# A hybrid block on one Trainium2 core: inverse's products emitted later among the dense matmuls, and an output projection that holds three weight tiles

## The chip, the core and the metric

The kernel runs on one core of one Trainium2 chip. The engines have separate, in-order instruction streams: TensorE (PE in the profile, with its weight loads as PEld), VectorE (DVE), ScalarE (ACT), GpSimd (POOL) and SyncE (SP). Semaphores, set by a tile framework, make one stream wait for another. The metric is device microseconds of one execution. The time of this kernel is 1151.71 us, the median of three runs that lie between 1146.16 and 1154.17 us.

## What is computed

One layer for 512 tokens of width 1024: a pre-norm, three token mixers, a gated merge, an output projection with residual, and a squared-ReLU MLP with residual and a last norm. Cut to what matters here:

```python
h = rms_norm(x, norm1_g)
p = h @ w_in                      # 1024 -> 11520 columns
y_a = b_a * causal_dwconv(c_a * x_a)                 # short convolution
y_b = rg_lru(causal_dwconv(x_b)) * gelu(g_b)         # linear recurrence over tokens
# RWKV-7, 16 heads of 64; state carried over 8 chunks of 64 tokens
sa = state @ (-kk); state = state*w + sa (kk*a)^T + v k^T; y_t = state @ r
m = gate_a*y_a + gate_b*y_b + gate_c*y_c
x = x + m @ w_out                 # 1024 x 1024
h2 = rms_norm(x, norm2_g)
x = x + square(relu(h2 @ mlp_w1)) @ mlp_w2           # 1024 -> 4096 -> 1024
return rms_norm(x, final_g)
```

## The kernel before, in words

All float32 products are made of three matmuls of split operands (`mm3`, lines 166 to 169): a high part and a low part of weight and of data. A weight tile is 128 x 1024. `load_w` (line 132) fetches it on SP's queue into `raw` (two buffers), ScalarE casts it to `whi` (line 146) and VectorE makes `wlo` = `raw` - `whi` (line 103, the helper `tt`). `whi` and `wlo` have three buffers each, so a tile can be split only when the matmuls of the third tile before it are done. A projection of one weight tile is 24 matmuls of 128x512 on TensorE; these are called dense matmuls below.

The RWKV mixer works on four groups of four heads. For each group `krv` (line 415) makes keys, decays, receptances and values; `amat` (line 514) makes the small products between them within each chunk (`pA`, then the transposes `pB`); `inverse` (line 543) inverts 32 triangular blocks of 64 by 64. Two `v.transpose` (line 550) bring the blocks' halves into `Z`, 31 steps of two short VectorE operations each (`dg` and `Z`, lines 559 and 561) invert the diagonal 32 by 32 blocks, two more transposes (line 567) and one (line 572) bring the result into the layout that TensorE needs, and 32 + 32 small matmuls (`pG`, line 577, and `pT`, line 587, in blocks of 16) make the off-diagonal part. Line 569 yields NINV times ahead of line 572, so that other work is emitted in between.

Everything else of the input projection (the branches `ab`, line 734: 8 times 7 weight tiles and the recurrences) is filler: a generator `fl` that `weave` (line 813) advances by a given number of steps for each step of the critical generator. The order in which instructions are emitted, with the priority offsets that `tc.high_priority` sets (CP, CPI and so on), is what the framework's scheduler turns into one fixed order on each engine. A matmul emitted under `pin` keeps its emission order and has a high priority.

After the last inverse the recurrence over eight chunks runs (`chain`, line 618), with the rest of the filler and the gates (`gate`, line 716) between its steps. Then `fin_m` (line 698) merges the branches, four steps for the first 256 tokens and four for the rest: for each of two row blocks q it makes `ym`, its high part `mh` (ScalarE) and its low part `ml` (VectorE). `w_out(th)` (line 873) multiplies them with the eight tiles of `w_out`, once for each half of the tokens, 24 matmuls of 128x256 for a tile and half; `to_tokens` (line 887) transposes the residual stream back and stores it. The MLP follows (`p`, then `acc` with `ah`).

Of the kernel before, what the change touches and what calls it, by code (L numbers as in the profile page):

```python
# [18 lines left out]
P = 128  # L19

OFF, OFFS, OFFP = 160, 20, 30
CP, CPI, CPK, CPC, CPN = 150, 60, 0, 20, 5
HOT = 6000

NINV, NG_T, N_LOAD = 16, 4, 6


N_INV, N_KRV = 41, 22
F_INV, F_KRV, F_GAP = 29, 14, 5
R0, R2, R3, R4 = 0.85, 0.8, 1.6, 1.0  # L30
NWARM = 2
POOL_KT = (1, 3, 5, 6, 7)
S = 512
# [64 lines left out]
def block_kernel(ctx, tc, xt, win, par, mulr, sw, wout, w1, w2, fg, cst, eyes, out):  # L98
# [3 lines left out]
    def tt(o, a, b, op):  # L102
        return v.tensor_tensor(out=o, in0=a, in1=b, op=op)  # L103
# [410 lines left out]
    def amat(g, G_):  # L514

        G_.AX = p1.tile([P, 2, NC, 4, L], F32, tag="AXt", name="AXt")
        for c4 in range(2):
            pts = four_banks("pA")
            for i in range(16):
                ci, jj, h = i // 4, 1 - i // 2 % 2, i % 2  # L520
                c = 4 * c4 + ci
                rows = slice(64 * h, 64 * h + 64)
                pin(i, lambda: pe.matmul(pts[2 * h + jj][:, ci], G_.BK[rows, jj, c], G_.AR[rows, jj, c],  # L523
                                 start=True, stop=True))
            for e in range(4):
                tt(G_.AX[:, :, 4 * c4:4 * c4 + 4, e], pts[e].rearrange("p c (a t) -> p a c t", a=2),
                   mask.rearrange("p (a t) -> p a t", a=2).unsqueeze(2).to_broadcast([P, 2, 4, L]), MUL)
            yield
        gp.dma_start(axd[:, 0:64, g, 1].rearrange("c s e t -> s c (e t)"),
                     G_.AX[0:64, 1].rearrange("s c e t -> s c (e t)"))  # L530
        for a in range(2):
            gp.dma_start(axd[:, 64:128, g, a].rearrange("c s e t -> s c (e t)"),
                         G_.AX[64:128, a].rearrange("s c e t -> s c (e t)"))
        BKT = p1.tile([P, NC, 2, P], F32, tag="BKT", name="BKT")
        for c2, pt in enumerate(four_banks("pB")):
            for i in range(4):
                c, jj = 2 * c2 + i // 2, i % 2
                pin(c2 + i, lambda: pe.transpose(pt[:, i], G_.BK[:, jj, c].rearrange("p a t -> p (a t)"), ident))
            ac.copy(BKT[:, 2 * c2:2 * c2 + 2].rearrange("p c j t -> p (c j) t"), pt)
        gp.dma_start(bkd[:, :, g].rearrange("c p j x -> p c (j x)"), BKT.rearrange("p c j x -> p c (j x)"))  # L540
        yield

    def inverse(g, G_):
        AXt = G_.AX
        Z = p1.tile([P, 2, 32, 32], F32, tag="Z", name="Z")
        la, xt = Z[64:128, 0], Z[64:128, 1]
        dg = p1.tile([P, 32, 32], F32, tag="dg", name="dg")
        tmp = dg[64:128].rearrange("p a b -> p (a b)")
        for b in range(2):
            v.transpose(la[32 * b:32 * b + 32].rearrange("l s t -> l t s"),  # L550
                        AXt[32 * b:32 * b + 32, 0, :, :, 32 * b:32 * b + 32].rearrange("s c e t -> s t (c e)"))
        gp.dma_start(xt.rearrange("l s t -> l (s t)"), eyes)

        yield
        yield
        for s in range(31):
            n, c = 31 - s, s + 1
            tv = tmp[:, 0:n * c].rearrange("l (c t) -> l c t", c=c)
            tt(tv, la[:, s, s + 1:32].unsqueeze(1).to_broadcast([64, c, n]),
               xt[:, 0:c, s:s + 1].to_broadcast([64, c, n]), MUL)  # L560
            tt(xt[:, 0:c, s + 1:32], xt[:, 0:c, s + 1:32], tv, ADD)
# [10 lines left out]
        v.transpose(d1[0:32], TT[0:32, :, 0:32])  # L572
        for half in range(2):
            pg = pm.tile([P, 16, 32], F32, tag="pm", name="pG")
            for i in range(16):
                l = 16 * half + i
                pin(i, lambda: pe.matmul(pg[32:64, i], AXt[0:32, 0, l // 4, l % 4, 32:64], d1[0:32, l],  # L577
                                             start=True, stop=True))
            ac.copy(gs[32:64, 16 * half:16 * half + 16], pg[32:64])
            yield  # L580
        for _ in range(NG_T):
            yield 0
        for half in range(2):
            pg = pm.tile([P, 16, 32], F32, tag="pm", name="pT")
            for i in range(16):
                l = 16 * half + i
                pin(i + half, lambda: pe.matmul(pg[0:32, i], gs[32:64, l], TT[32:64, l, 32:64], start=True, stop=True))
# [221 lines left out]
    def chainit(*gens):  # L809
        for x_ in gens:  # L810
            yield from x_
# [28 lines left out]
    pk_ctx.close()  # L840
# [12 lines left out]
    def fill_chain():  # L853
# [14 lines left out]
            yield  # L868
        yield from fin_m(0, 4)
        M["half"] = True  # L870
        yield from w_out(0)

    def w_out(th):
        tl = slice(th * HT, (th + 1) * HT)
        for mo in range(KT):
            w = load_w(wout[mo])
            acc = pp.tile([P, S], F32, tag="pp", name="acc")[:, 0:HT]
            for q in range(KT):
                mm3(acc, *wslice(w, q), GQ[q][th], BV[q][th], start=q == 0, stop=q == KT - 1)
            x2 = M["x2T"][:, mo, tl]  # L880
            tt(x2, acc, x2, ADD)
            hi = M["h2h"][:, mo, tl]
            ac.activation(hi, x2, AF.Copy, scale=pv("n2", mo))
            stt(M["h2l"][:, mo, tl], x2, pv("n2", mo), f(hi), MUL, SUB)
            yield

    def to_tokens(th):
# [195 lines left out]
```

## Time and profile before

| | |
|---|---|
| median of three runs | 1151.71 us (1146.16 to 1154.17) |
| the profiled execution | 1150.43 us, span of its instructions 1148.7 us |
| granted TensorE clock, mean | 0.955 |
| busy: TensorE, VectorE, ScalarE, GpSimd | 1071.1, 753.9, 484.2, 107.6 us |
| first pA of group 1 to the last pT of group 4 | about 86 to 592 us |
| chain over chunks | about 607 to 715 us |
| merge and output projection | about 724 to 789 us |
| MLP | about 789 to the end |

A row of the waits reads: engine, tile and line that waited, what released it, then us in total, times, longest. A row of the windows reads: the stretch in us from the span's start, its length, then busy us and number of instructions of TensorE, its weight loads, VectorE, ScalarE and GpSimd, the granted TensorE clock, the DMA engines' busy share and GB/s. A row of the timeline reads: start, duration, engine, line, operation, tiles; in brackets the idle time before it and what ended it. The profiler lists a small float32 matmul (pA, pG, pT) as two records, so 32 records of pG are a block of 16.

### The profile page before, as it was taken

To read this page: it belongs to the slowest core of one execution; us is meant where nothing else is said; L and a number is where in the kernel's file an instruction comes from. 1 tells how busy PE (TensorE), PEld (TensorE's weight loads), DVE (VectorE), ACT (ScalarE), POOL (GpSimd) and SP (SyncE) were. 2 spreads that over 40 slices of the span, in tenths; PEclk is the share of its full clock that TensorE was granted. 3 is DMA by queue.
4 is the path that set the end of the run, shared out by engine and by line. 5 is a ranking of instruction groups with operands and counts; after the bars stand their busy time and mean duration, and the time that the engine had idled before them with its cause. 6 is when DMAs were issued, how large, how long until landed. Compare 5 with 4: busy or idle time off the path is not lost.

```text
span 1148.7 us, 16170 instructions
## 1 busy us (share of the span) xinstructions
PE 1071.1 (93%) x6396; PEld 875.9 (76%) x6396; DVE 753.9 (66%) x1300; ACT 484.2 (42%) x714; POOL 107.6 (9%) x167
## 2 busy tenths in 40 slices
PE   8899969999699996999878999789999999999997
PEld 4677857788577875778667888689888888888885
DVE  7997967879579894898955777966544444222224
ACT  6645335444265451554525444355433433211123
POOL 3211001110011100001012220100000000000001
PEclk9999969999699996999979999889999999999999
DMA  6244414463234622436239873355333225323331
GB/s 207 81 126 123 149 55 114 114 158 116 59 99 140 173 78 80 115 114 175 76 110 288 265 236 116 129 177 182 101 97 105 92 93 178 115 92 95 107 92 73
DMA packets 44475, 146.32 MB, mean 127 GB/s; under 512 B 5808, under 2 KB 9392, under 8 KB 43376
## 3 DMA queue, kind: packets, MB, share of 16 engines
q1 hardware_dynamic: 30624, 95.21, 26.3%
q0 software_dynamic: 13056, 49.03, 14.9%
q8 instruction: 50, 0.82, 0.3%
q10 hardware_dynamic: 720, 1.05, 0.2%
q14 instruction: 25, 0.20, 0.1%
HBM read 120.11 MB, written 25.17 MB: 126 GB/s over the span
## 4 chain that ended last, share of the span: by engine, by line
PE 53%; DVE 10%; issue 7%; DMA 2%; ACT 1%; POOL 1%; ACTq 0%; POOLq 0%; DVEq 0%; SPq 0%
PE acc L167 6%; PE acc L168 6%; PE acc L169 6%; PE p L168 5%; PE p L167 5%; PE p L169 5%; PE pp L167 4%; PE pp L169 4%; PE pp L168 4%; DVE wlo L103 2%; DMA rt<-rtd 2%; PE py L644 1%; DVE dg L103 1%; DVE Z L103 1%; PE pA L523 1%
## 5 line engine op out<-in xcount | busy, mean ns | idle before, releaser
L103 DVE TENSOR_TENSOR wlo<-raw,whi 128x1024 fp32r<-128x1024 f32 (+1 forms) x172 | 209.5, 1219 | 274.1 <-ACT whi L146 260.4
L146 ACT CAST whi<-raw 128x1024 fp32r<-128x1024 f32 (+1 forms) x172 | 178.0, 1036 | 342.3 <-PE acc L169 126.2
L167 PE MATMUL pp<-hh,whi 128*128 128x512 f32 x696 | 270.9, 403 | 4.0 <-ACT g L747 1.1
L169 PE MATMUL pp<-hh,wlo 128*128 128x512 f32 x696 | 268.7, 400 | 4.2 <-DVE wlo L103 4.2
L168 PE MATMUL pp<-hl,whi 128*128 128x512 f32 x696 | 267.9, 399 | 2.8 <-DVE hl L106 2.8
L167 PEld LDWEIGHTS pp<-hh,whi 128*128 128x128 f32 x696 | 133.3, 192 | 36.0 <-ACT hh L291 1.5
L169 PEld LDWEIGHTS pp<-hh,wlo 128*128 128x128 f32 x696 | 133.3, 192 | 34.5 <-DVE wlo L103 6.0
L168 PEld LDWEIGHTS pp<-hl,whi 128*128 128x128 f32 x696 | 133.5, 192 | 31.5 <-DVE hl L106 3.2
L169 PE MATMUL p<-h2h,wlo 128*128 128x512 f32 (+1 forms) x264 | 101.2, 383 | 0.0
L167 PE MATMUL p<-h2h,whi 128*128 128x512 f32 (+1 forms) x264 | 101.1, 383 | 0.0
L168 PE MATMUL p<-h2l,whi 128*128 128x512 f32 (+1 forms) x264 | 101.0, 383 | 0.0
L167 PE MATMUL acc<-whi,ah 128*128 128x512 f32 x256 | 99.6, 389 | 0.0
L168 PE MATMUL acc<-wlo,ah 128*128 128x512 f32 x256 | 99.6, 389 | 0.0
L169 PE MATMUL acc<-whi,al 128*128 128x512 f32 x256 | 99.6, 389 | 0.0
L169 PEld LDWEIGHTS p<-h2h,wlo 128*128 128x128 f32 x264 | 49.6, 188 | 9.7
L167 PEld LDWEIGHTS p<-h2h,whi 128*128 128x128 f32 x264 | 49.6, 188 | 9.6
L168 PEld LDWEIGHTS p<-h2l,whi 128*128 128x128 f32 x264 | 49.6, 188 | 9.5
L168 PEld LDWEIGHTS acc<-wlo,ah 128*128 128x128 f32 x256 | 48.0, 188 | 10.1
L169 PEld LDWEIGHTS acc<-whi,al 128*128 128x128 f32 x256 | 48.0, 188 | 10.1
L167 PEld LDWEIGHTS acc<-whi,ah 128*128 128x128 f32 x256 | 48.0, 188 | 9.8
L577 PE MATMUL pG<-dg,AXt 32*32 32x32 f32 x256 | 14.7, 236 | 36.5 <-DVE dg L572 36.5
L103 DVE TENSOR_TENSOR dg<-Z 64x31 f32<-64x31 f32 (+15 forms) x124 | 42.2, 340 | 4.1
(296 smaller groups left out, 1519.9 us busy)
## 6 DMA issues: line engine op xcount, KB each, us to landing
raw<-in_win SPq DMA_DIRECT2D x88, 512.0 KB, 3.5
raw<-in_w SPq DMA_DIRECT2D x64, 512.0 KB, 3.5
ax<-axd POOLq DMA_DIRECT2D x8, 1024.0 KB, 8.0
raw<-in_wout SPq DMA_DIRECT2D x16, 512.0 KB, 3.5
axd<-AXt POOLq DMA_DIRECT2D x12, 512.0 KB, 7.4
bkd<-BKT POOLq DMA_DIRECT2D x4, 1024.0 KB, 13.9
bk<-bkd POOLq DMA_DIRECT2D x7, 512.0 KB, 9.5
swr<-in_sw SPq DMA_DIRECT2D x16, 128.0 KB, 2.3
```

The lines of the kernel that those rows point to most:

```text
L103: return v.tensor_tensor(out=o, in0=a, in1=b, op=op)
L146: ac.copy(hi[:, sl], raw[:, sl])
L167: pe.matmul(ps, wh, xh, start=start, stop=False)
L168: pe.matmul(ps, wh, xl, start=False, stop=False)
L169: pe.matmul(ps, wl, xh, start=False, stop=stop)
L523: pin(i, lambda: pe.matmul(pts[2 * h + jj][:, ci], G_.BK[rows, jj, c], G_.AR[rows, jj, c], start=True, stop=True))
L577: pin(i, lambda: pe.matmul(pg[32:64, i], AXt[0:32, 0, l // 4, l % 4, 32:64], d1[0:32, l], start=True, stop=True))
L644: pin(behind, lambda: pe.matmul(py[64 * h:64 * h + 64, x], w, y, start=first and x == 0, stop=last, skip_group_check=True))
```

## The change

Two things are changed. In the RWKV groups, the last transpose of `inverse` (`d1`) is emitted ahead of the yields and not behind them, there are 19 yields instead of 16, and they have no extra priority. Keys and filler of the next group are now one generator, `fill_group`, that runs beside the inverse (1.15 steps for each of its steps) and is drained behind it; before, the inverse ran beside filler alone and `krv` followed. All small matmuls of `pA` are pinned, the first one too. In the output projection, three weight tiles are held: `w_out_first` multiplies them with the first half of the tokens, into the left half of three PSUM tiles, and `w_out_rest` with the second half; the five other tiles are loaded once and multiplied with both halves. `to_tokens(0)` comes after that. So eight loads and splits of weight tiles go, and the additions behind the projection are 512 tokens wide.

```diff
-CP, CPI, CPK, CPC, CPN = 150, 60, 0, 20, 5
+CP, CPI, CPK, CPC, CPN = 150, 0, 0, 20, 5
-NINV, NG_T, N_LOAD = 16, 4, 6
-N_INV, N_KRV = 41, 22
-F_INV, F_KRV, F_GAP = 29, 14, 5
-R0, R2, R3, R4 = 0.85, 0.8, 1.6, 1.0
+NINV, NG_T, N_LOAD = 19, 4, 6
+N_KRV = 22
+F_INV, F_KRV, F_GAP = 22, 16, 4
+W3 = 3
+R0, R1, R2, R3, R4 = 0.85, 1.15, 1.1, 1.7, 1.0
...
-                pin(i, lambda: pe.matmul(pts[2 * h + jj][:, ci], G_.BK[rows, jj, c], G_.AR[rows, jj, c],
+                pin(True, lambda: pe.matmul(pts[2 * h + jj][:, ci], G_.BK[rows, jj, c], G_.AR[rows, jj, c],
...
+        d1 = gs = dg
+        v.transpose(d1[0:32], TT[0:32, :, 0:32])
         for _ in range(NINV):
             yield CPI
-        d1 = gs = dg
-        v.transpose(d1[0:32], TT[0:32, :, 0:32])
...
+    def fill_group(g):
+        for _ in range(F_INV):
+            next(fl, None)
+            yield
+        acc = 0.0
+        for _ in krv(g, GS[g]):
+            yield
+            acc += F_KRV / N_KRV
+            while acc >= 1.0:
+                acc -= 1.0
+                next(fl, None)
+                yield
+        for _ in range(F_GAP):
+            next(fl, None)
+            yield
...
         if g:
-            weave(inverse(g - 1, GS[g - 1]), fl, F_INV / N_INV)
-            weave(krv(g, GS[g]), fl, F_KRV / N_KRV, CPK)
-            for _ in range(F_GAP):
-                next(fl, None)
+            fgr = fill_group(g)
+            weave(inverse(g - 1, GS[g - 1]), fgr, R1)
+            drain(fgr)
...
-        yield from w_out(0)
+        yield from w_out_first()
...
+    def w_out_mm(mo, w, acc, th):
+        for q in range(KT):
+            mm3(acc[:, HALF[th]], *wslice(w, q), GQ[q][th], BV[q][th], start=q == 0, stop=q == KT - 1)
+    def w_out_first():
+        M["w"], M["acc"] = [], []
+        for mo in range(W3):
+            w = load_w(wout[mo])
+            acc = pp.tile([P, S], F32, tag="pp", name="acc")
+            w_out_mm(mo, w, acc, 0)
+            M["w"].append(w)
+            M["acc"].append(acc)
+            yield
+    def w_out_rest():
+        for mo in range(W3):
+            w_out_mm(mo, M["w"][mo], M["acc"][mo], 1)
+            w_out_end(mo, M["acc"][mo])
+            yield
+        for mo in range(W3, KT):
+            w = load_w(wout[mo])
+            acc = pp.tile([P, S], F32, tag="pp", name="acc")
+            for th in range(2):
+                w_out_mm(mo, w, acc, th)
+            w_out_end(mo, acc)
+            yield
...
+    drain(w_out_rest())
     drain(to_tokens(0))
-    drain(w_out(1))
```

What the scheduler makes of it is seen in the order of the instructions. Line numbers of the changed kernel are one higher from line 30 on, 571 is the `d1` transpose, and later ones are up to 39 higher. Numbers behind a name tell buffers of one name apart.

TensorE, the first group's inverse, before: the end of the dense matmuls in front of the first `pG`. `pp_1466` and `pp_1486` are two projections, each with its own `whi` and `wlo`.

```order
L167 MATMUL pp_1466<-hh_73,whi_1461 128x512
L167 MATMUL pp_1486<-hh_73,whi_1481 128x512
L168 MATMUL pp_1466<-hl_74,whi_1461 128x512
L168 MATMUL pp_1486<-hl_74,whi_1481 128x512
L169 MATMUL pp_1466<-hh_73,wlo_1462 128x512
L169 MATMUL pp_1486<-hh_73,wlo_1482 128x512
L167 MATMUL pp_1466<-hh_73,whi_1461 128x512
L167 MATMUL pp_1486<-hh_73,whi_1481 128x512
L577 MATMUL pG_1306<-dg_1038,AXt_927 32x32 x16
```

The same engine and place in the changed kernel: the 182nd to 187th dense matmul behind the last `pB`.

```order
L170 MATMUL pp_1414<-hh_73,wlo_1410 128x512
L168 MATMUL pp_1428<-hh_73,whi_1423 128x512
L169 MATMUL pp_1428<-hl_74,whi_1423 128x512
L170 MATMUL pp_1428<-hh_73,wlo_1424 128x512
L168 MATMUL pp_1428<-hh_73,whi_1423 128x512
L169 MATMUL pp_1428<-hl_74,whi_1423 128x512
```

And the `pG` block of the changed kernel, behind 260 dense matmuls:

```order
L170 MATMUL pp_1545<-hh_73,wlo_1541 128x512
L168 MATMUL pp_1545<-hh_73,whi_1540 128x512
L169 MATMUL pp_1545<-hl_74,whi_1540 128x512
L170 MATMUL pp_1545<-hh_73,wlo_1541 128x512
L578 MATMUL pG_1564<-dg_1038,AXt_927 32x32 x16
L168 MATMUL pp_1513<-hh_73,whi_1508 128x512
```

The small matmuls moved back by 78 dense ones in this group, and dense ones now stand between their blocks.

VectorE at the end of the same inverse, before:

```order
L103 TENSOR_TENSOR wlo_1482<-raw_1480,whi_1481 128x1024
L103 TENSOR_TENSOR Z_1037<-Z_1037,dg_1038 64x28x4
L103 TENSOR_TENSOR dg_1038<-Z_1037 64x87
L103 TENSOR_TENSOR Z_1037<-Z_1037,dg_1038 64x29x3
L103 TENSOR_TENSOR dg_1038<-Z_1037 64x60
L103 TENSOR_TENSOR Z_1037<-Z_1037,dg_1038 64x30x2
L103 TENSOR_TENSOR dg_1038<-Z_1037 64x31
L103 TENSOR_TENSOR Z_1037<-Z_1037,dg_1038 64x31
L567 STREAM_TRANSPOSE Z_1037<-Z_1037 32x32x32 x2
L572 STREAM_TRANSPOSE dg_1038<-Z_1037 32x1024
L103 TENSOR_TENSOR wlo_1541<-raw_1539,whi_1540 128x1024
```

and in the changed kernel:

```order
L104 TENSOR_TENSOR Z_1037<-Z_1037,dg_1038 64x30x2
L104 TENSOR_TENSOR dg_1038<-Z_1037 64x31
L104 TENSOR_TENSOR Z_1037<-Z_1037,dg_1038 64x31
L568 STREAM_TRANSPOSE Z_1037<-Z_1037 32x32x32 x2
L571 STREAM_TRANSPOSE dg_1038<-Z_1037 32x1024
L104 TENSOR_TENSOR wlo_1424<-raw_1422,whi_1423 128x1024
L107 SCALAR_TENSOR_TENSOR u1_1163<-u3_1353,u1_1163 128x512
L104 TENSOR_TENSOR swbl_2146<-swr_2143,swbh_2145 128x256
L104 TENSOR_TENSOR wlo_1509<-raw_1507,whi_1508 128x1024
```

The place of the transposes hardly moved; `wlo_1424`, which the 185th dense matmul reads, stands right behind the last of them.

TensorE in the output projection of the changed kernel, where the three held tiles end (`acc_6505`, `acc_6555` with the second half) and the fourth tile begins:

```order
L170 MATMUL acc_6555<-mh_6607,wlo_6551 128x256
L168 MATMUL acc_6555<-mh_6614,whi_6550 128x256
L169 MATMUL acc_6555<-ml_6615,whi_6550 128x256
L170 MATMUL acc_6555<-mh_6614,wlo_6551 128x256
L168 MATMUL acc_6705<-mh_6345,whi_6700 128x256
L169 MATMUL acc_6705<-ml_6346,whi_6700 128x256
L931 MATMUL tp_6989<-ident_63,x2T_6332 128x128 x2
L168 MATMUL acc_6763<-mh_6345,whi_6758 128x256
L169 MATMUL acc_6763<-ml_6346,whi_6758 128x256
L170 MATMUL acc_6705<-mh_6345,wlo_6701 128x256
```

Ahead of this row stand 144 matmuls of the three held tiles with both halves; before, the fifth tile's matmuls with the first half stood behind 96.

More of the change, by code (lines that the diff above doesn't have):

```diff
@@ L870, in fill_chain, with w_out_end @@
         M["half"] = True
-        yield from w_out(0)
-    def w_out(th):
-        tl = slice(th * HT, (th + 1) * HT)
-        for mo in range(KT):
-            w = load_w(wout[mo])
[L877 to L884, printed above, removed]
+        yield from w_out_first()
+    def w_out_mm(mo, w, acc, th):
+        for q in range(KT):
+            mm3(acc[:, HALF[th]], *wslice(w, q), GQ[q][th], BV[q][th], start=q == 0, stop=q == KT - 1)
+    def w_out_end(mo, acc):
+        x2 = M["x2T"][:, mo]
+        tt(x2, acc, x2, ADD)
+        hi = M["h2h"][:, mo]
+        ac.activation(hi, x2, AF.Copy, scale=pv("n2", mo))
+        stt(M["h2l"][:, mo], x2, pv("n2", mo), f(hi), MUL, SUB)
+    def w_out_first():
+        M["w"], M["acc"] = [], []
+        for mo in range(W3):
+            w = load_w(wout[mo])
+            acc = pp.tile([P, S], F32, tag="pp", name="acc")
[14 more added lines that the diff above has]
+            w_out_end(mo, acc)
             yield
```

## The prediction

> **What bounds the kernel now.** The page of the profile comes first: busy times, and the slices of the span for TensorE and its granted clock.
>
> ```profile
> span 1148.7 us, 16170 instructions
> PE 1071.1 (93%) x6396; PEld 875.9 (76%) x6396; DVE 753.9 (66%) x1300; ACT 484.2 (42%) x714; POOL 107.6 (9%) x167
> ...
> PE   8899969999699996999878999789999999999997
> ...
> PEclk9999969999699996999979999889999999999999
> ```
>
> TensorE is busy for 93% of the span, so what can be won is its idle time and the time that it runs at a low clock. Both dip together, in slices 6, 11, 16 and 20 to 21 (28.7 us each): once for each group of heads. A later, smaller dip is at the output projection (slices 26 and 27). The waits of TensorE name the causes, first over the span, then in a window around each inverse.
>
> ```profile
> PE pG L577 <- DVE dg L572: 36.5, 4, 11.2
> PE acc L167 <- ACT whi L146: 4.8, 1, 4.8
> ```
> ```profile
> PE pG L577 <- DVE dg L572: 5.3, 1, 5.3
> PE pp L169 <- DVE wlo L103: 3.9, 1, 3.9
> ...
> PE pG L577 <- DVE dg L572: 9.3, 1, 9.3
> ...
> PE pp L169 <- DVE wlo L103: 0.2, 1, 0.2
> ...
> PE pG L577 <- DVE dg L572: 11.2, 1, 11.2
> ...
> PE pG L577 <- DVE dg L572: 10.7, 1, 10.7
> ```
>
> So the four inverses cost 9.2, 9.5, 11.2 and 10.7 us of waiting, 40.6 in all. The windows from each inverse's first transpose to its first `pG` show who is late: VectorE is busy for 49.42 of 52.25 us and so on, 209 of 221 us in the four, and most of the rest is the small gaps between dependent steps. While it inverts, VectorE is the bound.
>
> ```profile
> 106.70:158.95 52.25, 43.05 (x190) 34.85 (x187) 49.42 (x89) 17.14 (x24) 3.54 (x5) 0.93 0.45 126
> 244.20:301.50 57.30, 46.76 (x210) 37.98 (x208) 54.23 (x97) 24.39 (x35) 3.55 (x5) 0.94 0.41 118
> 384.00:440.40 56.40, 45.28 (x199) 36.74 (x197) 53.34 (x96) 23.52 (x33) 2.79 (x4) 0.92 0.45 128
> 525.40:580.40 55.00, 44.29 (x197) 36.31 (x195) 51.99 (x95) 23.30 (x33) 3.38 (x5) 0.95 0.42 112
> ```
>
> The waits have an echo. From the first `pG` on, TensorE is busy, but at half its clock (the column 0.50 or 0.51):
>
> ```profile
> 158.95:175.75 16.80, 16.77 (x149) 13.70 (x150) 6.29 (x9) 9.63 (x16) 0.71 (x1) 0.51 0.23 62
> 301.50:315.80 14.30, 14.27 (x145) 12.20 (x146) 1.77 (x2) 3.93 (x6) 0.72 (x1) 0.51 0.28 72
> 440.45:452.00 11.55, 11.55 (x138) 10.09 (x139) 3.06 (x4) 2.92 (x5) 0.72 (x1) 0.50 0.27 67
> 580.40:588.60 8.20, 8.18 (x75) 7.15 (x76) 4.27 (x6) 2.46 (x4) 0.55 (x1) 0.50 0.47 158
> ```
>
> What that costs, from the timeline: ten dense matmuls take 2.27 us at full clock (0.227 each), six take 2.56 at half clock (0.427). A block of 16 small ones takes 1.84 us (164.11 to 165.95) against 1.13 (589.02 to 590.15).
>
> ```profile
> 144.09 0.39 PE L167 MATMUL pp<-hh,whi 128*128 128x512 f32 x1
> ...
> 146.36 0.39 PE L168 MATMUL pp<-hl,whi 128*128 128x512 f32 x1
> ...
> 164.11 1.91 PE L577 MATMUL pG<-dg,AXt 32*32 32x32 f32 x32
> 165.95 0.80 PE L168 MATMUL pp<-hl,whi 128*128 128x512 f32 x1
> ...
> 585.41 0.63 PE L167 MATMUL pp<-hh,whi 128*128 128x512 f32 x1
> ...
> 587.97 0.63 PE L167 MATMUL pp<-hh,whi 128*128 128x512 f32 x1
> ...
> 589.02 1.19 PE L587 MATMUL pT<-Z,dg 32*32 32x32 f32 x32
> 590.15 0.50 PE L167 MATMUL pp<-hh,whi 128*128 128x512 f32 x1
> ```
>
> The first three stretches hold four blocks each, the last two. Blocks lose 0.71 us each (14 of them, 9.9 us); the remaining 50.85 - 14 x 1.84 = 25.1 us are dense work, of which 47% is lost (1 - 0.227/0.427), 11.8 us. Together 21.7. The inverses cost 40.6 + 21.7 = 62 us.
>
> **The change part by part: idle at the inverses.** By its numbers the move is enough: 260, 260, 260 and 241 dense matmuls stand between the last `pB` and the first `pG`, where 182, 198, 200 and 194 stood; 47 to 78 more at 0.227 are 10.7 to 17.7 us, at or above the waits. But the order shows a second thing. Those matmuls read a `wlo`, and VectorE's order was not moved with them. In the first group the 185th dense matmul reads `wlo_1424`, which VectorE makes behind the last transpose; in the other groups it is the 211th, 198th and 226th. The wait at `pG` becomes a wait at a dense matmul. I cost each as a difference to the wait of before: minus what VectorE no longer does ahead of the transposes, plus one `wlo` behind them, minus the dense matmuls won. VectorE's rows for that:
>
> ```profile
> L103 DVE TENSOR_TENSOR wlo<-raw,whi 128x1024 fp32r<-128x1024 f32 (+1 forms) x172 | 209.5, 1219 | 274.1 <-ACT whi L146 260.4 <-issue 12.5
> ...
> L106 DVE SCALAR_TENSOR_TENSOR u<-u,part,u 128x511 f32<-128x511 f32 (+2 forms) x24 | 17.9, 745 | 4.3 <-ACT u L740 3.8
> ...
> L784 DVE TENSOR_TENSOR_SCAN u<-u,u 128x512 f32<-128x512 f32 x8 | 9.8, 1223 | 0.2
> ...
> L103 DVE TENSOR_TENSOR u<-u,g 128x512 f32<-128x512 f32 x8 | 5.5, 690 | 7.2 <-ACT u L773 7.1
> ```
>
> - Group 1: one `wlo`, one scan and two operations of 0.69 fewer (3.8 us), 184 for 182 matmuls (0.5): 9.2 - 3.8 + 1.2 - 0.5 = 6.1.
> - Group 2: two `wlo` fewer (2.4), 210 for 198 (2.7): 9.5 - 2.4 + 1.2 - 2.7 = 5.6.
> - Group 3: a `wlo`, a scan, two of 0.745 and two of 0.69 fewer (5.3), one of 0.69 more behind the transposes, 197 for 200 (-0.7): 11.2 - 5.3 + 1.9 + 0.7 = 8.5.
> - Group 4: nearly the same VectorE work (-0.3), 225 for 194 (7.0): 10.7 - 0.3 + 1.2 - 7.0 = 4.6.
>
> That is 24.8 us for 40.6: 15.8 won. Bounds: VectorE's work that left the inverse must still be done before the next one, so at the low end only the matmuls of groups 2 and 4 count (9.7 less 4.9 for four `wlo`: 5); at the high end 21, were the last `wlo` made ahead of the transposes.
>
> **The clock behind the wait.** After the new wait dense matmuls follow, and the blocks of 16 come one by one, 5 to 35 dense matmuls apart. How long dense work takes to bring the clock back shows where the last block of before ended and where its half-clock stretch ended:
>
> ```profile
> 309.84 0.72 PE pp L167
> ...
> 448.76 0.72 PE pp L167
> ```
>
> 309.84 to 315.80 and 448.76 to 452.00 are 6.0 and 3.2 us. I take 4.6, which loses 2.2 us at 47%, four times: 8.7 for 21.7, 13 won. Bounds: 5 (a second wait per group lets the clock fall again, 2.2 us four times) and 21.7 (it never falls). The Trainium skill ("TensorE: Matmul & The Clock Gate", section "Part 1: The HAM clock gate") gives one window of about 3.4 us of activity for the way back; by that the loss is an estimated 1.6 us each and the whole time 2 us less than mine. Rows of 3.2 and 6.0 scatter around and above it.
>
> **New waits.** The keys of the next group now start inside the inverse's tail, so TensorE meets their short products (`pn`, two in `krv`, which need VectorE's split) earlier. Between the inverses VectorE has room (the first and the last of the three stretches):
>
> ```profile
> 158.95:244.20 85.25, 83.70 (x484) 66.80 (x485) 59.48 (x106) 39.56 (x58) 9.79 (x16) 0.90 0.36 104
> ...
> 440.40:525.40 85.00, 83.99 (x501) 67.76 (x502) 60.52 (x106) 40.96 (x61) 9.19 (x15) 0.93 0.37 106
> ```
>
> It is busy for about 60 of 85 us there. In the new order TensorE has 254 dense matmuls from `wlo_1424` to the next `pA` (57.7 us), some 5 us of small blocks and 2.2 of low clock, 65 us. VectorE fits, with 5 us to spare after the `wlo` it has to make up. I take 6 us for waits at `pn` and at a late `wlo` (1.5 per group); ends 0 and 16, the latter if half of the 25 us that VectorE itself stands still there comes to bear in two groups. The POOL queue carries `ttd`, the next `eyes` load and the keys' stores in another order; 28 us of dense work lie between the last `pT` and the next `pA`, against a few us of transfers, so nothing is charged.
>
> **The output projection.** Before, its matmuls run from 728.12 to 789.3 (a window of TensorE alone: busy, count, clock, DMA); the one large wait in it is explained by the chain:
>
> ```profile
> 728.12:789.30 61.18, 54.90 (x419) 0.91 0.50 164
> ```
> ```profile
> 745.91 3.48 DMA raw<-in_wout
> 749.49 1.05 ACT whi L146
> 750.54 0.55 PE acc L167
> ```
>
> VectorE is filled with `fin_m`, makes the third and fourth tile's `wlo` late, and only then does `raw` come free for the fifth load. With three held tiles, 144 matmuls need no new load while `fin_m` runs, so of the 6.3 us of idle (61.18 - 54.90) the 4.8 go, 1 of the smaller waits for a `wlo`, and the clock dip behind them (2.2): 8. Eight casts and eight `wlo` and 4 MB of loads go too, on engines that were not the bound: nothing. Against that: the fourth tile can be cast only when the first held one is done, ten matmuls ahead (10 x 54.9/419 = 1.3 us), while two additions of 0.69 and a `wlo` take 2.6: 1.3 lost. The eight token blocks come in one row, each copy waiting for a store, beside the 48 half matmuls of the first MLP tile (48 x 0.13 = 6.3 us): 0.7. That is 6 won; ends 1 (the row of blocks waits) and 10.
>
> **The sum.** 15.8 + 13 - 6 + 6 = 28.8. The profiled execution took 1150.4 us (span 1148.7 and 1.7 around it): 1121.6. The median of 1151.7 is 1.3 above it: 1123.
>
> **Rivals.**
> 1. The change does what its numbers say: VectorE gets far enough ahead, nobody waits at the inverses. 40.6 + 21.7 + 6 = 68 off: 1084. For it: 260 dense matmuls against 182. Against: `wlo_1424` behind the transposes.
> 2. Nothing measurable: VectorE paces the whole period, its 25 us of standstill stay, and what left the inverse comes back behind it. Then the last group and the projection alone win, about half of 6.1 and 6: 1146. For it: in the inverse VectorE is at 95%. Against: 30% free after it.
> 3. Slower: TensorE's strict order meets VectorE's chain of keys at five places per group (two `pn`, a late `wlo` each, the `wlo` behind the transposes), each a wait of 3.9 (the row of `wlo`) and a clock dip of 2.2: 30 us for three groups, 7 in the last, 97 for 62: 35 slower, 6 off for the projection: 1181. It decides from about 3.3 waits per group ((62 + 6 - 7)/(3 x 6.1)). Against: I count one long wait and short ones. The Trainium skill names this pattern in the same page, section "HAM oscillation": repeated gaps above one window drop the clock again and again. The dips at each inverse agree with it; four or five per group no run here shows.
>
> **The numbers.** Forecast 0.64, rival 1 0.10, rival 2 0.16, rival 3 0.10. The forecast's own ends are 5 + 5 - 16 + 1, which is no gain, and 21 + 21.7 + 10; not all ends fall together, and I take 14 to 42 off: 1110 to 1138. To leave out no more than 2 in 10, the range reaches over most of rival 2: 1104 to 1149. A change under 1% (11.5 us) can hardly be told from none here. Faster by more: forecast and rival 1 and a little of rival 2, 0.76; within: 0.15; slower: 0.09.
>
> **What would show it.** Right: no wait of `pG` on `dg`, but waits of `pp` L170 on `wlo`, four long ones of 4 to 9 us; the half clock for 3 to 6 us behind each, with dense matmuls; no wait for `raw` of `wout`; a projection of about 55 us. Wrong: `pp` waits of over 12 us a group, waits of `pn` of several us, or a clock row without dips at all.

## The result, and the profile after

The changed kernel takes 1120.97 us (median of four runs, 1119.94 to 1121.97), the kernel before 1148.93 us beside it: a ratio of 0.975, 95% interval 0.971 to 0.980. It is faster by 28 us; the forecast was 1123 us. The profiled execution took 1119.94 us, 30.5 less than that of before, and the terms below are compared with that.

The head of its page: busy times, the slices of TensorE and its granted clock.

```profile
span 1118.2 us, 16117 instructions
...
PE 1055.3 (94%) x6396; PEld 863.6 (77%) x6396; DVE 746.4 (67%) x1276; ACT 473.4 (42%) x698; POOL 108.0 (10%) x167
...
PE   8899979999699979999898999899999999999997
...
PEclk8999989999899989999999999999999999999999
```

TensorE does the same 6396 instructions in 15.8 us less of busy time, and is still idle in about as many places: slices 6, 11 and 15, and weakly at 20. The clock row has lost its sixes and sevens. The waits over the span say what became of `pG`:

```profile
PE pp L170 <- DVE wlo L104: 21.5, 4, 7.7
PE pn L433 <- ACT bh L163: 10.2, 4, 8.8
PE py L645 <- DMA rt<-rtd: 4.2, 1, 4.2
```

No `pG` waits for `dg` any more. In its place a dense matmul waits for `wlo` in three groups and the short product of the keys, `pn`, in one (its releaser `bh` is what ScalarE makes from VectorE's `ks`). The timeline has the five long waits (idle time and releaser in brackets):

```profile
158.67 0.80 PE L170 MATMUL pp<-hh,wlo 128*128 128x512 f32 x1 [7.66 <-DVE wlo L104]
...
290.93 0.80 PE L433 MATMUL pn<-bh,bd 128*128 128x512 f32 x1 [8.76 <-ACT bh L163]
...
413.43 0.79 PE L170 MATMUL pp<-hh,wlo 128*128 128x512 f32 x1 [6.67 <-DVE wlo L104]
...
512.08 0.50 PE L170 MATMUL pp<-hh,wlo 128*128 128x512 f32 x1 [2.40 <-DVE wlo L104]
...
547.38 0.79 PE L170 MATMUL pp<-hh,wlo 128*128 128x512 f32 x1 [4.78 <-DVE wlo L104]
```

VectorE at the first of them: two transposes, the third, and only then the split that TensorE waits for, which ends (158.6) as TensorE starts (158.67).

```profile
152.41 3.83 DVE L568 STREAM_TRANSPOSE Z<-Z 32x1024 f32<-32x1024 f32 x2
156.27 1.23 DVE L571 STREAM_TRANSPOSE dg<-Z 32x1024 f32<-32x1024 f32 x1
157.44 1.17 DVE L104 TENSOR_TENSOR wlo<-raw,whi 128x1024 fp32r<-128x1024 f32 x1
```

Windows from each inverse's first transpose to the end of its long wait (the first and the last of four) show VectorE busy for 46.75 of 50.23 us and so on, 203 of 222 in the four: it is still the bound there.

```profile
108.44:158.67 50.23, 42.57 (x193) 34.99 (x191) 46.75 (x86) 19.58 (x28) 3.55 (x5) 0.96 0.43 121
...
486.17:547.38 61.21, 54.04 (x234) 43.90 (x232) 53.05 (x96) 24.81 (x37) 3.55 (x5) 0.97 0.38 104
```

Behind the waits, the stretches at half clock (column 0.50 to 0.61; the fourth is the one behind the wait of 2.40):

```profile
158.67:164.70 6.03, 6.03 (x14) 4.77 (x15) 5.22 (x8) 4.78 (x8) 0.00 (x0) 0.50 0.59 197
290.93:294.60 3.67, 3.67 (x9) 2.92 (x10) 3.27 (x7) 1.38 (x2) 0.00 (x0) 0.52 0.32 88
413.43:420.70 7.27, 6.44 (x14) 4.62 (x15) 5.48 (x11) 1.34 (x2) 0.00 (x0) 0.50 0.48 144
511.90:516.30 4.40, 4.22 (x12) 3.30 (x13) 4.15 (x9) 0.56 (x1) 0.00 (x0) 0.61 0.44 123
547.38:550.60 3.22, 3.21 (x8) 2.58 (x9) 1.95 (x4) 2.60 (x4) 0.00 (x0) 0.53 0.57 179
```

That is some 22.8 us of busy time at half clock (taking 3.5 of the fourth), 47% of it lost: 10.7 us, against 21.7 before.

One stage was not looked at for the prediction, from the first `pA` of a group to its last `pB`. Here it is for group 2, before and then after.

```profile
228.84:245.45 16.61, 16.61 (x123) 13.41 (x124) 11.39 (x18) 6.64 (x10) 2.66 (x6) 1.00 0.38 124
```
```profile
225.29:234.07 8.78, 8.78 (x92) 7.64 (x92) 6.94 (x11) 2.68 (x5) 0.53 (x1) 1.00 0.24 76
```

Before, the timeline has 35 dense matmuls among the small ones; after, 11. Taken off at 0.227 us each, the small products cost 8.7 us before and 6.3 after. Over the four groups, idle time left out, it is 34.6 us before and 25.8 after, 8.8 less. Not all of that was won. The windows of before also hold `pV`, the transposes of the values, eight records a group; after, `pV` stands ahead of the first `pA`, outside the windows. There it costs 0.9 to 1.1 us a group (in group 2 a block of four takes 0.36 us, from 219.07 to 219.43, and the dense matmul behind it 0.09 more; there are two blocks), 3.9 us in all. So 4.9 us were won and 3.9 only moved. TensorE's busy time bears this out: of the 15.8 us that it lost, 11.0 are the clock's, which leaves less than 5 for everything else.

The projection's window, and the MLP's first layer of before and of after:

```profile
702.85:757.21 54.36, 51.97 (x408) 50.58 (x409) 38.91 (x81) 18.27 (x31) 2.70 (x4) 0.97 0.32 107
```
```profile
789.62:966.20 176.58, 176.47 (x810) 146.99 (x809) 84.67 (x105) 72.16 (x106) 2.17 (x4) 1.00 0.35 108
```
```profile
757.21:935.72 178.51, 178.47 (x824) 148.39 (x822) 86.19 (x107) 74.01 (x112) 4.39 (x8) 1.00 0.33 106
```

The projection is 7.1 us shorter (61.5 before, in the window that ends with its last matmul), and 2.5 us more go in the transposes ahead of it (6.5 to 4.0 from the first `pYt` to the first `acc`). The MLP's first layer, which now has the token blocks and half matmuls at its start, is 1.9 us longer.

### The profile page after: what moved, and what is told of

Same layout as the page of the kernel before. It is cut to its first block, busy times and chain, and to the rows that moved or that the text cites. A ratio compares the mean times of both kernels' runs of the same rounds, so it can differ in the third digit from the quotient of the medians.

```text
span 1118.2 us, 16117 instructions
## 1 busy us (share of the span) xinstructions
PE 1055.3 (94%) x6396; PEld 863.6 (77%) x6396; DVE 746.4 (67%) x1276; ACT 473.4 (42%) x698; POOL 108.0 (10%) x167
## 4 chain that ended last, share of the span: by engine, by line
PE 61%; DVE 27%; issue 5%; DMA 4%; ACT 3%; POOL 1%; SPq 0%; DVEq 0%; POOLq 0%; ACTq 0%
PE pp L168 7%; PE pp L170 6%; PE pp L169 6%; PE acc L170 6%; PE acc L168 6%; PE acc L169 6%; PE p L168 5%; PE p L170 5%; PE p L169 5%; DVE wlo L104 5%; DVE Z L104 3%; DVE dg L104 3%; DVE g L107 2%; DMA rt<-rtd 2%; DVE u L107 2%
## 5 line engine op out<-in xcount | busy, mean ns | idle before, releaser
L104 DVE TENSOR_TENSOR wlo<-raw,whi 128x1024 fp32r<-128x1024 f32 (+1 forms) x164 | 199.6, 1218 | 249.6 <-ACT whi L147 247.9
L147 ACT CAST whi<-raw 128x1024 fp32r<-128x1024 f32 (+1 forms) x164 | 169.6, 1035 | 318.6 <-PE acc L170 126.3
L170 PE MATMUL pp<-hh,wlo 128*128 128x512 f32 x696 | 278.1, 400 | 21.6 <-DVE wlo L104 21.5
L168 PE MATMUL pp<-hh,whi 128*128 128x512 f32 x696 | 278.6, 401 | 4.1 <-ACT g L804 1.5
L169 PE MATMUL pp<-hl,whi 128*128 128x512 f32 x696 | 276.6, 397 | 2.8 <-DVE hl L107 2.8
L169 PEld LDWEIGHTS acc<-wlo,ah 128*128 128x128 f32 x256 | 48.0, 188 | 10.1
L104 DVE TENSOR_TENSOR dg<-Z 64x31 f32<-64x31 f32 (+15 forms) x124 | 42.2, 340 | 4.1
L104 DVE TENSOR_TENSOR Z<-Z,dg 64x31 f32<-64x31 f32 (+15 forms) x124 | 42.2, 340 | 4.1
```

Of the source, the lines that this page charges most:

```text
L147: ac.copy(hi[:, sl], raw[:, sl])
L168: pe.matmul(ps, wh, xh, start=start, stop=False)
L169: pe.matmul(ps, wh, xl, start=False, stop=False)
L170: pe.matmul(ps, wl, xh, start=False, stop=stop)
```

## The experiments

The theory from the prediction: VectorE is the bound in each inverse, and what TensorE waits for is a `wlo` behind the three transposes; the low clock behind a wait is a cost of its own. The rivals: VectorE paces the whole period, so that a wait removed comes back elsewhere; or the gain is not where the sum put it (another part of the change, the projection). The kernel before took 1150 to 1152 us (medians) beside these runs.

**The two parts alone.** The group part with the old projection:

```diff
-R0, R1, R2, R3, R4 = 0.85, 1.15, 1.1, 1.7, 1.0
+R0, R1, R2, R3, R4 = 0.85, 1.15, 1.1, 1.6, 1.0
...
-        yield from w_out_first()
+        yield from w_out(0)
...
-    drain(w_out_rest())
     drain(to_tokens(0))
+    drain(w_out(1))
```

> The changed kernel with the output projection of before (two passes over the eight tiles, R3 = 1.6). Theory A, the prediction's sum: the group part is worth 15.8 + 13 - 6 = 22.8 us, and the two traces agree with it as far as they can be lined up (the first product of the chain comes 24.3 us earlier), so 1125 to 1127 us. Rival B, the two parts need each other (the late groups only pay because the projection's loads find the queue free): a gain well under 20 us, 1132 or more.

Measured: 1128.52 us (1126.33 to 1131.19), ratio 0.981 (0.977 to 0.985): 23.1 us, against 22.8 by the sum, while the kernel is 1.5 us above the expected range. Its waits at the inverses are those of the whole change to 0.1 us (window over the four inverses):

```profile
PE pp L170 <- DVE wlo L104: 21.5, 4, 7.6
PE pn L433 <- ACT bh L163: 9.9, 3, 8.8
```

And the projection alone, the same edit the other way round in the kernel before.

> The kernel before with the new output projection alone (three tiles held, R3 = 1.7). Theory A: 6 us by the prediction, 7 by the lengths of the projection in the two traces (61.5 and 54.4) less 1.9 in the MLP behind it, so 1142 to 1144 us, with no wait for whi in the projection. Rival B: the saved loads were hidden, 1148 to 1149.

Measured: 1138.95 us (1134.55 to 1146.56), ratio 0.989 (0.985 to 0.993). That is 8 to 18 us by the times, more than the 6 to 7 expected. (These 8 to 18 are the interval; the medians differ by 12.7.) Its trace shows no such gain: the projection takes 53.3 us for 61.5, the transposes ahead of it 0.6 less, the MLP's first layer 2.2 more, 6.6 us in all; its other stages are those of before within 1.7 us each, and the whole execution is 3.9 us shorter than the profiled one of before.

```profile
730.32:783.58 53.26, 52.62 (x408) 51.54 (x409) 36.46 (x78) 17.51 (x30) 2.71 (x4) 0.94 0.33 110
```

The profiled execution was the slowest of the four (1146.56), and runs of kernels with the old group part scatter by 9 to 12 us, those with the new one by 0.6 to 5.5. By its trace the projection is worth 7 us, which the times neither confirm nor refute; that 23.1 and 12.7 sum to more than the 30.5 of both together lies within that scatter.

**The pin at `pA`.** The changed kernel, with the first product unpinned as before:

```diff
-                pin(True, lambda: pe.matmul(pts[2 * h + jj][:, ci], G_.BK[rows, jj, c], G_.AR[rows, jj, c],
+                pin(i, lambda: pe.matmul(pts[2 * h + jj][:, ci], G_.BK[rows, jj, c], G_.AR[rows, jj, c],
```

> The changed kernel with the first small product of pA no longer pinned, as before. In the traces the stretch from pA to pB holds 8.7 to 9.5 us beside its dense matmuls before and 6.2 to 9.2 after, some 7 us in all, a gain that the prediction did not price. If the pin makes it: about 1128 us, and dense matmuls again between the small products of pA. If the order of emission makes it (keys and branches drained ahead of pA): 1121 as the changed kernel.

Measured: 1115.73 us (1114.28 to 1119.78), ratio 0.970 (0.967 to 0.974): neither answer. The stretch from `pA` to `pB` is long again, with 78 dense matmuls in group 2:

```profile
204.28:231.77 27.49, 26.38 (x166) 21.41 (x167) 20.08 (x29) 11.04 (x17) 4.54 (x9) 1.00 0.40 126
```

So the pin does make the short stretches, and undoing it costs 5.1 us in the four (34.8 us without idle time and with `pV`, for 25.8 and the 3.9 of `pV`). But the waits at the inverses fall by more; in the window over the four of them:

```profile
PE pp L170 <- DVE wlo L104: 21.0, 4, 8.6
...
PE pn L433 <- ACT bh L163: 0.5, 2, 0.3
```

9.9 us of `pn` became 0.5. What the pin wins at the small products it more than gives back in waits: without it the kernel is 5.2 us faster than the changed one. Why is only argued: 41 to 84 more dense matmuls between `pA` and `pB` give VectorE time to get ahead.

**The third transpose behind the yields again.**

```diff
         d1 = gs = dg
-        v.transpose(d1[0:32], TT[0:32, :, 0:32])
         for _ in range(NINV):
             yield CPI
+        v.transpose(d1[0:32], TT[0:32, :, 0:32])
```

> The changed kernel with the last transpose of the inverse behind the yields again. In VectorE's order the wlo that TensorE waits for then stands ahead of that transpose (1.23 us) in group 1 and behind it no more in the others. Theory A (the wait ends with the wlo behind the transposes): each of the four waits is shorter by about 1.2 us, and little else changes: 1115 to 1117 us. Rival B (something else ends last, or the products wait for the transpose instead): 1121 or more, with a wait of pG for dg.

Measured: 1116.99 us (1116.60 to 1117.17), ratio 0.971 (0.968 to 0.974), at the upper end of theory A, but for its reason only in part. In the window over the inverses three waits are for `wlo`, one is now for `ks`, a product of VectorE for the keys, and the one of `pn` in group 2 is as long as before:

```profile
PE pp L170 <- DVE wlo L104: 12.8, 3, 6.6
PE pp L168 <- DVE ks L107: 9.1, 1, 9.1
PE pn L433 <- ACT bh L163: 9.1, 2, 8.8
```

The wait in group 1 is 6.6 for 7.7 us, and the long one in group 4 3.8 for 4.8, as theory A has it. In group 3 moving one split let the next product of VectorE end last: `ks`, for 9.1 us where `wlo` had cost 6.7. Together these waits are 31.0 us for 31.4, so their length did not make the gain. TensorE's busy time fell, from 1055.3 to 1051.9 us; the half clock behind the wait of group 1, for one, lasts 3.5 us for 6.0. That the time came out where theory A put it is luck.

Then the changed kernel again beside three more.

> The changed kernel itself, so that the other three can be compared with it on one chip. 1119 to 1122 us if the chips agree; the first experiments then say that undoing the pin (1115.7) and moving the transpose (1117.0) are each worth about 4 to 5 us.

Measured: 1120.44 us (1119.28 to 1120.93), ratio 0.975 (0.970 to 0.979), as expected.

**Both undoings together.**

> The changed kernel with both small undoings: the first product of pA unpinned and the last transpose behind the yields. If their gains are of different waits (the pin's: VectorE makes wlo ahead while the small products of pA stand among dense ones; the transpose's: one wlo 1.2 us earlier): they add, about 1111 us. If both feed the same wait: 1115 to 1116 as the better one.

Measured: 1114.46 us (1112.66 to 1116.13), ratio 0.969 (0.965 to 0.973). This is 2.5 us below the transpose alone and 1.3 below the pin alone: of the 5.2 and 4.0 us that each gains alone, both together gain 6.0. They feed the same waits more than they add.

**VectorE's splits on GpSimd.**

```diff
+        NW["n"] += 1
+        if NW["on"] and NW["n"] % 1 == 0:
+            gp.tensor_tensor(out=lo[:, sl], in0=raw[:, sl], in1=f(hi[:, sl]), op=SUB)
+        else:
+            tt(lo[:, sl], raw[:, sl], f(hi[:, sl]), SUB)
-        tt(lo[:, sl], raw[:, sl], f(hi[:, sl]), SUB)
...
+        NW["on"] = True
...
+        NW["on"] = False
```

> The changed kernel, with every wlo that is emitted between the start of an inverse and its pG made by GpSimd and not by VectorE: 40 splits in all, the order of TensorE as it was. GpSimd is busy for 3 to 5 of 70 us there, and its products of 128x512 took 1.26 and 1.92 us, so a split of 128x1024 is an estimated 2.5 to 3.8 us, under the 5.45 us that TensorE needs for a tile. VectorE loses some 8 splits of 1.17 us, 9.4 us, ahead of each last transpose. Theory A (rival 1 of the prediction: VectorE's late wlo is what is left at the inverses): the waits of pp for wlo go, 33 us of idle and 10.7 us of low clock less what the keys' pn still costs, 1080 to 1095 us. Theory B (another product of VectorE is late next): half of it, 1100 to 1110, with waits of pn or of pp for a tile that VectorE frees. Theory C (GpSimd's own time or its sharing of memory with VectorE costs more): pp waits for GpSimd or VectorE's steps get longer, 1121 or more.

Measured: 1147.96 us (1146.43 to 1149.88), ratio 0.999 (0.997 to 1.001). The whole gain is gone; theory C. GpSimd and VectorE in the first inverse, from the two timelines:

```profile
140.29 2.44 POOL L152 TENSOR_TENSOR wlo<-raw,whi 128x1024 fp32r<-128x1024 f32 x1 [2.46 <-ACT whi L149]
150.55 2.72 POOL L152 TENSOR_TENSOR wlo<-raw,whi 128x1024 fp32r<-128x1024 f32 x1 [7.82 <-ACT whi L149]
...
160.78 2.45 POOL L152 TENSOR_TENSOR wlo<-raw,whi 128x1024 fp32r<-128x1024 f32 x1 [1.97 <-ACT whi L149]
```
```profile
140.42 2.59 DVE L104 TENSOR_TENSOR Z<-Z,dg 64x247 f32<-64x247 f32 x1
143.04 0.41 DVE L104 TENSOR_TENSOR dg<-Z 64x240 f32<-64x240 f32 x1
...
151.02 2.43 DVE L104 TENSOR_TENSOR dg<-Z 64x156 f32<-64x156 f32 x1
153.48 0.32 DVE L104 TENSOR_TENSOR Z<-Z,dg 64x156 f32<-64x156 f32 x1
...
158.92 4.31 DVE L575 STREAM_TRANSPOSE Z<-Z 32x1024 f32<-32x1024 f32 x2
```

A step of the inverse that takes 0.41 or 0.32 us takes 2.59 or 2.43 when a split of GpSimd is under way: it ends 0.2 to 0.3 us behind the split. Two transposes that overlap a split of 2.45 us take 4.31 us for 3.83, 0.5 longer. So a split cost VectorE 1.22 us when it did it, and 2.1 to 2.2 us in these two steps when GpSimd did. Over the kernel, in the groups of lines, the first operation of the inverse's steps grew from 42.2 us to the 65.1 of this row, and the second from 42.2 to 64.5.

```profile
L104 DVE TENSOR_TENSOR dg<-Z 64x31 f32<-64x31 f32 (+15 forms) x124 | 65.1, 525 | 4.2
```

That is 45 us more on the chain that bounds the inverse, against 48.5 us of splits taken away (199.6 to 151.1 in VectorE's group of `wlo`). Other operations of VectorE got longer too: in all it is busy for 763.4 us where it was 746.4, so it was not relieved at all. TensorE waits 17.1 us for `wlo` tiles of GpSimd, and its idle time over the kernel is 81.9 us for 62.9. The Trainium skill ("SBUF — State Buffer", section "Who interferes with whom") states that a VectorE instruction with two inputs in SBUF is fully blocked while a GpSimd instruction that reads SBUF holds the port they share, and that one with at most one input there, outside the modes that use both ports, does not contend. The rows above agree with the first half, and but for those 0.5 us with the second.

With the two undoings on top:

> The two undoings and the splits on GpSimd together. Theory A: with no late wlo at the inverses the undone pin has nothing left to win there and costs what it costs at pA (about 7 us in the traces), so no better than the splits on GpSimd alone, 0 to 7 us slower. Theory B (other products of VectorE are late): the undone pin still gives VectorE room, 3 to 6 us faster than the splits on GpSimd alone.

Measured: 1162.64 us (1161.16 to 1163.04), ratio 1.011 (1.007 to 1.015): 14.7 us slower than the splits on GpSimd alone, outside both expectations, which rested on the splits being a gain.

**VectorE relieved without GpSimd.** The same 40 splits, with a copy by ScalarE in their place:

```diff
-            gp.tensor_tensor(out=lo[:, sl], in0=raw[:, sl], in1=f(hi[:, sl]), op=SUB)
+            ac.copy(lo[:, sl], raw[:, sl])
```

> The changed kernel with the 40 splits of the inverses taken from VectorE and not given to GpSimd: in their place ScalarE writes a second copy of raw into wlo (1.03 us by its row for whi), so the low parts of those weights are left out of the computation. TensorE's order stays as it was. Theory A (VectorE's work is what TensorE waits for at the inverses, and its splits are 49 us of it): the waits of pp for wlo and of pn go and the clock stays up, up to 33 + 10.7 us: 1077 to 1090 us. Theory B (TensorE meets the next late product at once: keys, branches, ScalarE, which gets 41 us more): 1095 to 1110. Theory C (TensorE's waits are not VectorE's doing): 1118 or more. The difference to the run with the splits on GpSimd (1148) is then what GpSimd's way of doing them cost.

Measured: 1094.52 us (1094.18 to 1097.56), ratio 0.952 (0.949 to 0.954), 26 us below the changed kernel: between theory A's range and B's, and half a microsecond from B's. TensorE waits for `wlo` nowhere at the inverses; in the window over them the largest are

```profile
PE pn L439 <- ACT bh L169: 7.4, 3, 6.2
PE pp L174 <- DVE ks L107: 4.1, 1, 4.1
```

both products of VectorE, or of ScalarE behind it. So VectorE's work is what TensorE waits for (theory C falls), the splits are most of it, and the next late thing is the keys. VectorE's two operations of the inverse's steps take 42.2 us each, as in the changed kernel. The 53 us between this run and the one on GpSimd are what the splits cost on GpSimd rather than on ScalarE, which blocks nobody here.

**VectorE's order alone.** Nothing is taken away; the transposes are put behind the split that was emitted last (`behind` orders the two on VectorE, without a wait):

```diff
+        for _ in range(16):
+            yield CPI
...
-            v.transpose(TT[32 * b:32 * b + 32, :, 32 * b:32 * b + 32].rearrange("s l t -> s t l"),
+            behind(v.transpose(TT[32 * b:32 * b + 32, :, 32 * b:32 * b + 32].rearrange("s l t -> s t l"),
...
+        for _ in range(3):
+            yield CPI
         d1 = gs = dg
         v.transpose(d1[0:32], TT[0:32, :, 0:32])
-        for _ in range(NINV):
-            yield CPI
```

> The changed kernel with an order on VectorE: the two transposes into Z's other half are put behind the wlo that was split last (16 of the 19 yields ahead of them), the last transpose behind them. In groups 1 to 3 the wlo that TensorE waits for and the next one then stand ahead of all three transposes, in group 4 one of them between. Theory A (the wait is the 5.1 us of transposes ahead of the wlo): each wait is 4 to 5 us shorter, and short enough for the clock to stay up: 17 us of idle and some 8 of low clock, 1095 to 1100 us. Theory B (VectorE is behind with all of its work up to the next keys, whatever its order): the waits move to a later wlo, a pn or pG for dg, 1112 to 1120, no better than with the last transpose alone behind (1117).

Measured: 1106.99 us (1106.78 to 1108.35), ratio 0.962 (0.960 to 0.965): 13.5 us below the changed kernel, between the two theories. In the first group VectorE now does

```profile
152.15 1.23 DVE L104 TENSOR_TENSOR wlo<-raw,whi 128x1024 fp32r<-128x1024 f32 x1
...
154.24 1.22 DVE L104 TENSOR_TENSOR wlo<-raw,whi 128x1024 fp32r<-128x1024 f32 x1
155.48 2.10 DVE L577 STREAM_TRANSPOSE Z<-Z 32x1024 f32<-32x1024 f32 x1
```

and over the inverses TensorE waits for

```profile
PE pn L440 <- ACT bh L170: 8.6, 4, 5.4
PE pp L177 <- DVE wlo L104: 6.4, 4, 2.4
PE pp L175 <- DVE ks L107: 5.2, 1, 5.2
```

The waits for `wlo` went from 21.5 to 6.4 us: that much of theory A holds. But 5.2 us come back at `ks`, and the `pn` of the keys keeps its 8.6: the part of B that holds. With the first `pA` unpinned as well:

> The same order on VectorE with the first pA unpinned, beside 1114.5 us for the unpinned kernel with only the last transpose moved. Theory A: 5 to 10 us faster than that, 1105 to 1110. Theory B: the same, 1113 to 1117.

Measured: 1102.70 us (1100.34 to 1104.15), ratio 0.958 (0.955 to 0.961); 11.8 us below the unpinned kernel with only the last transpose moved, a little more than theory A gave. In the window over the inverses its waits are

```profile
PE pp L177 <- DVE wlo L104: 5.4, 3, 3.6
PE pn L440 <- ACT bh L170: 2.6, 4, 1.2
```

This kernel computes all that the changed one does, and is the fastest of those that do: 18 us below the changed kernel, 48 below the kernel before.

**The clock by itself.** Repeated dense matmuls fill the time in which TensorE would wait in group 4:

```diff
+    NPR, EXTRA = [], {70: 8, 71: 18}
...
+        NPR.append(name)
+        for _ in range(EXTRA.get(len(NPR) - 1, 0)):
+            pe.matmul(t, wslice(w, 0)[0], hh[:, 0], start=True, stop=True)
```

> The changed kernel with 8 and 18 repeated dense matmuls (the first product of the tile, done again, 1.8 and 4.1 us) ahead of the two tiles whose wlo TensorE waits for in group 4 (2.4 and 4.8 us). VectorE's and ScalarE's orders are the same. If the low clock behind a wait is a cost of its own: the two stretches at half clock of 3.3 and 3.2 us go, 1.5 us each, and the stretch from the last pB to the last pT of group 4 falls from 81.3 to about 78.3 us, although TensorE does more. If VectorE paces it: 81 us again, with a new wait, or more.

Measured: 1120.50 us (1119.48 to 1120.88), ratio 0.974 (0.971 to 0.977); the stretch from the last `pB` to the last `pT` of group 4 takes 80.6 us for 81.3, not 78.3. The eight matmuls missed their place: the wait of 2.4 us and the low clock behind it are still there. At the other wait the experiment works. The same seven microseconds in it and in the changed kernel:

```profile
545.00:552.00 7.00, 7.00 (x49) 5.63 (x48) 5.72 (x8) 3.48 (x6) 0.00 (x0) 1.00 0.25 84
```
```profile
545.00:552.00 7.00, 4.62 (x14) 3.71 (x15) 5.73 (x8) 3.20 (x5) 0.00 (x0) 0.76 0.27 87
```

No wait, and the clock at 1.00. The stretch's sum: 26 more matmuls at 0.227 (5.9 us), 4.8 us less idle, so 1.1 us more; it came out 0.7 us shorter. So 1.8 us are the clock's, for one stretch of 3.2 us at half clock (1.5 expected). Here the low clock is a cost of its own, and no new wait took its place. This is one stretch of one execution; the kernel as a whole is no faster than the changed one (1120.50 for 1120.44).

## Why the prediction was right, and where it was not

The mechanism held: the wait at `pG` became a wait of a dense matmul for the `wlo` behind the last transpose, at the tile that the order named, with VectorE as the bound (rows of the timeline; the run with VectorE relieved and the run with its order changed). The sum was nearly right partly by luck, because its errors cancel: waits and clock cost 4.5 us more than I had, and 4.9 us that I had not priced were won at the small products. Term by term, on the profiled executions:

| term | predicted | measured |
|---|---|---|
| idle at the inverses, new waits included | 40.6 to 24.8 + 6 = 30.8 | 40.6 to 33.3 (7.7, 10.1, 8.3, 7.2) |
| lost to the low clock | 21.7 to 8.7 | 21.7 to 10.7 |
| small products from `pA` to `pB` | not priced | 4.9 won |
| output projection, with the transposes ahead of it and the MLP's start | 6 won | 7.1 + 2.5 - 1.9 = 7.7 won |
| the rest | 0 | 0.4 lost |
| sum | 28.8 | 30.5 |

- **Idle at the inverses.** By group I had 6.1, 5.6, 8.5 and 4.6 us. Group 3 came out at 6.7 for `wlo` (8.3 with two small waits). In group 4 there were two waits for `wlo`, 2.4 and 4.8: I had looked at the `wlo` behind the transposes only, not at the one ahead of them. In group 2 the wait is 8.8, and not where I put it: TensorE stands at `pn`, which is ahead of the `wlo` in its order and needs `ks`, made by VectorE behind that `wlo`. A wait of `pn` of several us was on my list of what would make the prediction wrong. It makes one term wrong: I priced the keys' early start as four small waits beside the long ones, and in one group it is the long one. Together the waits are 2.5 us above my 30.8. (The 33.3 counts small waits too, 1.3 us for `g` in group 2 among them; the 40.6 leaves out one of 1.1 for `g` in the same group.)
- **The clock.** 2.2 us for each of four events, by 4.6 us of half clock. There were five events, since a wait of 2.4 us was enough for one; the stretches were 6.0, 3.7, 6.4, about 3.5 and 3.2 us. The two of 3.2 and 6.0 that I read in the trace of before were nearly the bounds. The window of about 3.4 us of the Trainium skill ("TensorE: Matmul & The Clock Gate", section "Part 1: The HAM clock gate") was nearer in three of five cases, and would have given an estimated 1.6 us for each of the five, 8.0.
- **`pA`.** I had the pin in the diff and no price for it. It wins about 5 us at the small products, as the traces and the undone pin show, and the undone pin shows too that the kernel is 5 us faster without it. It is not a free gain of the change, and the term belongs to the waits it helps to cause.
- **The projection.** The 4.8 us load wait and the clock behind it went as described; the length (54.4 us, "about 55") came out. Its price ahead of the MLP was low: 1.9 us for 0.7. Of the 2.5 us in the transposes ahead of it the run with the projection alone shows only 0.6, so the rest may belong to the other part.
- **The rest** holds the chain over the chunks, 1.5 us longer (a wait of 4.2 for `rt`), and 1.5 us more idle time between `pA` and `pB` (2.4 for 1.0); against them the 1.1 us for `g` and small differences that the traces don't settle.

Rival 1 (all waits go, 1084 us) did not come: even the run that took the splits away reached only 1094.5 and still waited for the keys. Rival 2 was half right: VectorE does pace what follows, as the `ks` and `pn` waits show when a `wlo` is moved ahead, but two thirds of the wait for `wlo` did not come back. Rival 3 needed four or five long waits a group; there were one or two.

## What to carry to other kernels

Two engines with fixed orders meet at every tile they exchange. If only one order is moved, the wait moves to the next tile that the other engine makes late; so look for that tile, and move the long instructions of the other engine behind it. Here, 5 us of transposes put behind two splits were worth half as much as the whole change. An engine's bound is not relieved by a neighbour that blocks it while it helps.

## What was not expected of the hardware

GpSimd's two-input work stops VectorE's two-input work for its whole length (0.4 us became 2.6), not for its share, while VectorE's transposes run beside it with little loss (4.31 us for 3.83; rows above).

A short wait can halve the clock. In the run with VectorE's order changed, the windows behind a wait of 2.43 us and behind one of 1.73 us:

```profile
501.70:506.20 4.50, 4.46 (x13) 3.54 (x14) 4.26 (x8) 0.81 (x1) 0.00 (x0) 0.66 0.37 120
534.00:538.50 4.50, 4.50 (x30) 3.51 (x31) 4.44 (x5) 1.27 (x2) 0.00 (x0) 1.00 0.40 117
```

The first holds 13 dense matmuls in 4.5 us, the second 17 and the first 13 records of a block of small ones. The Trainium skill ("TensorE: Matmul & The Clock Gate", section "HAM oscillation") speaks of gaps above about 3.4 us; here 2.4 us of idle time were enough. But the length of the wait does not decide it alone. One wait for the same product, `g`, stands in group 2 of two runs: of 1.88 us with the pin undone, with the clock at 1.00 over the 4.5 us behind it, and of 1.85 us with both undoings, with 0.62. In the fastest kernel a wait of 1.68 us was followed by 0.62 as well. What decides it besides the length these runs do not show.
